# Seven products of a two-by-two block multiplication: one bank each, or three banks that collect the sums, with copies in between

## The chip, the cores and the metric

The program runs on one core of a Trainium2 chip. The metric is the device time in microseconds (us) of one execution; the verdict compares the medians of several executions. TensorE (PE) multiplies, VectorE (DVE) and ScalarE (ACT) work elementwise, GpSimd (POOL) helps with sums and splits, SyncE (SP) issues the transfers. Each of these works through its own instructions strictly in order.

## What is computed

One layer of a decoder block over 1024 tokens of width 1024, in float32: a gated feed-forward block, a token mixer, a second feed-forward block, each behind an RMS norm whose shift, scale and gate come from a condition vector `c` ("adaLN", nine vectors). Only the three wide input projections matter here:

```
def swiglu(h, w_in, w_out):
    a, b = jnp.split(h @ w_in, 2, axis=-1)
    return (jax.nn.silu(a) * b) @ w_out
...
q, f, i, og, u, ga, gb = jnp.split(h @ w_in, IN_SPLITS, axis=-1)   # the mixer
...
u = ua * jax.nn.sigmoid(ub)                                         # its convolution branch
merged = jax.nn.sigmoid(ga) * y_a + jax.nn.sigmoid(gb) * y_b        # its gates
```

## The kernel before

Every float32 operand is split in two parts (`parts`): a high one, a cast by ScalarE (L90), and a low one, what is left, a subtraction by VectorE (L91). A product of 128 by 128 weights and 512 columns is three matmuls (`mmw`, L232 to L234): high by high, high by low, low by high.

`paired` computes the wide input projections `h @ w_in` of both feed-forward blocks and of the mixer's u, ga and gb columns. For one pair of column blocks f (128 columns of a and of b) and all 1024 tokens it is a two by two block product, done with seven multiplications in place of eight. Each of the seven is a `product` of 4 x 3 matmuls, 128x512 each. The first two f's of a loop (`fs`) are done in the plain way while the operands come in ("warm"); the other f's, 20 in each feed-forward block and 14 in the mixer, run one after the other.

- `prepare(f)`: SyncE loads two raw tiles (`ra`, 512 KB each); they are split and combined into seven weight operands w11, w12, w22, ws1 to ws4 in the pool `wp`. The combinations (L306, L251) are made in place in the raw tiles. `prepare` of the next f stands in the program ahead of the seven products of this f.
- The seven products p1 to p7 go to seven of the eight PSUM banks in turn. Between them stand one copy (L321, ScalarE, p1 into a tile u) and six sums on VectorE (L323 to L335), each of which reads one bank.
- `emit` makes the result: in a feed-forward block a Silu on ScalarE (L360) and a product on VectorE (L361); `after` makes seven operands for the second half of the block out of each pair of f's (`combos`, four differences on VectorE, L354, and seven stores).
- In feed-forward 1 `after` also works off the adaLN vectors ("mod", L154): 56 rows of the matrix `ada_w`, four for an f. Each is loaded by SyncE (L147, 512 KB, tiles `ada`) into the pool `rp` of **three** raw tiles, the same pool from which `ra` comes, and multiplied and summed by one VectorE instruction over 1024 columns, in place. Its tile is free again when that has run.
- In the mixer's loop `after` starts the convolution, 31 VectorE instructions over 1024 columns for each of two channel blocks.

The order of the instructions on each engine is set when the program is built, by priorities: an instruction has the priority of its place in the code, and `defer(n)` moves it back by n. The same scheduler picks the free tile of a pool. At run time nothing is reordered.

Of the kernel before, what the change touches and what calls it, by code (L numbers as in the profile page):

```python
# [22 lines left out]
NKK = 11  # L23
# [17 lines left out]
class Block:  # L41
# [19 lines left out]
    @contextmanager  # L61
    def defer(self, n):

        keep = self.tc.cur_priority
        self.tc.cur_priority = keep + n
        yield
        self.tc.cur_priority = keep


    def half(self):  # L70
# [155 lines left out]
        self.split(t[:, 0, :], t[:, 1, :], src, eng)  # L226
        return t

    def mmw(self, ps, w, i, x, first, last):
        wh, wl = w[:, 0, i * P:(i + 1) * P], w[:, 1, i * P:(i + 1) * P]  # L230
        mm = self.nc.tensor.matmul
        mm(ps, wh, x[:, 0, :], start=first, stop=False)  # L232
        mm(ps, wh, x[:, 1, :], start=False, stop=False)  # L233
        mm(ps, wl, x[:, 0, :], start=False, stop=last)  # L234

# [6 lines left out]
    def paired(self, ctx, h, hctx, src, order, warm, emit, after, right, ready=()):  # L242


        nc = self.nc
        V, A = nc.vector, nc.scalar
        sub, add = ALU.subtract, ALU.add
        fs = order[:2]

        def tt(dst, a, b):  # L250
            V.tensor_tensor(dst, a, b, op=sub)  # L251

        def load(f):
            rs = []
            for b in range(2):
                rs.append(self.rp.tile([P, D], F32, tag="raw", name=self.nm("ra")))
                nc.sync.dma_start(rs[b], src(f, b))
            return rs

        self.part(ctx, wp=11, hq=8, bq=4)  # L260
        wop = lambda x: self.parts(x, self.wp, "w")
        hq = lambda x: self.parts(x, self.hq, "hq")


        ws, banks, b1 = {}, {}, dict(ready)

        def warm_load(f):
            ws[f] = [[self.parts(r[:, i * T:(i + 1) * T], self.wp, "w", nc.gpsimd) for i in range(2)] for r in load(f)]

        def warm_parts(hh, k):  # L270
            if (hh, k) not in b1:
                b1[hh, k] = self.parts(h[1][k], self.bq, "bq") if hh == 1 and k < 4 else self.parts(h[hh][k])

        def warm_mm(f, hh, k):
            if k == 0:
                banks[f, hh] = [self.acc() if f == fs[0] else self.bank() for _ in range(2)]
            for b in range(2):
                self.mmw(banks[f, hh][b], ws[f][b][k // 4], k % 4, b1[hh, k], k == 0, k == NK - 1)

        def warm_end(hh):  # L280
            for f in fs:
                emit(f, hh, *banks[f, hh], None)

        warm(fs, warm_load, warm_parts, warm_mm, warm_end)
        b11, b21, b22 = ([b1[hh, k0 + i] for i in range(4)] for hh, k0 in ((0, 0), (0, 4), (1, 4)))
        t1, t2, t3, t4 = [], [], [], []
        for i in range(4):
            x11, x12, x21, x22 = h[0][i], h[1][i], h[0][4 + i], h[1][4 + i]
            for o, x, y in ((x11, x12, x11), (x12, x22, x12), (x22, x22, x11), (x21, x21, x22)):
                nc.gpsimd.tensor_tensor(o, x, y, op=sub)  # L290
            t2.append(hq(x22))
            t3.append(hq(x12))
            t1.append(self.parts(x11))
            t4.append(self.parts(x21, self.bq, "bq"))
        hctx.close()
        self.part(ctx, right=True, **right)

        def product(ps, w, xs):
            for i in range(4):
                self.mmw(ps, w, i, xs[i], i == 0, i == 3)  # L300

        def prepare(f):
            ra, rb = load(f)
            a11, a12, a21, a22 = ra[:, :T], ra[:, T:], rb[:, :T], rb[:, T:]
            w11, w12, w22 = wop(a11), wop(a12), wop(a22)
            V.tensor_tensor(a22, a21, a22, op=add)  # L306
            tt(a21, a11, a21)
            tt(a11, a22, a11)
            tt(a12, a12, a11)
            ws2, ws3, ws1, ws4 = wop(a11), wop(a21), wop(a22), wop(a12)  # L310
            return w11, w12, w22, ws1, ws2, ws3, ws4

        ops = None
        for n, f in enumerate(order):
            if f not in fs:
                w11, w12, w22, ws1, ws2, ws3, ws4 = ops if ops else prepare(f)
                ops = prepare(order[n + 1]) if n + 1 < len(order) else None
                p1, p2, p3, p4, p5, p6, p7 = [self.acc() if (7 * n + i) % 2 == 0 else self.bank() for i in range(7)]
                product(p1, w11, b11)
                c11, c21, c22, u = (self.piece() for _ in range(4))  # L320
                A.copy(u, p1)  # L321
                product(p2, w12, b21)
                V.tensor_tensor(c11, p2, u, op=add)  # L323
                product(p3, ws2, t2)
                V.tensor_tensor(u, p3, u, op=add)
                product(p4, ws3, t3)
                V.tensor_tensor(c22, p4, u, op=add)
                product(p5, w22, t4)
                V.tensor_tensor(c21, p5, c22, op=add)
                emit(f, 0, c11, c21, c21)  # L330
                product(p6, ws1, t1)
                V.tensor_tensor(c22, p6, c22, op=add)
                V.tensor_tensor(u, p6, u, op=add)
                product(p7, ws4, b22)
                V.tensor_tensor(u, p7, u, op=add)  # L335
                emit(f, 1, u, c22, c22)
            after(n, f)
        return b1

    def piece(self):  # L340
# [3 lines left out]
    def ffn(self, h, hctx, w_in, w_out, gate, warm, residual, norm, done, between=None):  # L344
# [6 lines left out]
        gs = {f: [] for f in order}  # L351

        def tt(dst, a, b):
            V.tensor_tensor(dst, a, b, op=sub)  # L354
# [1 line left out]
        def swiglu(f, hh, a, b, dst):  # L356
            s = self.half()
            if dst is None:
                dst = self.half()
            A.activation(s, a, AF.Silu)  # L360
            V.tensor_tensor(dst, b, s, op=ALU.mult)  # L361
            gs[f].append(dst)

        def combos(i):

            (x11, x12), (x21, x22) = gs[i], gs[NKK + i]
# [12 lines left out]
            put(6, c4)  # L379
# [12 lines left out]
        with ExitStack() as ctx:  # L392
# [54 lines left out]
            us = []  # L447
# [227 lines left out]
    def run(self):  # L675
# [113 lines left out]
        def mix_in(f, hh, x, y, dst):  # L789
            sx = x if dst is not None else self.half()  # L790
            A.activation(sx, x, AF.Sigmoid)
            if f >= NH:
                sy = y if dst is not None else self.half()
                A.activation(sy, y, AF.Sigmoid)
                for b, s in enumerate((sx, sy)):
                    nc.sync.dma_start(self.g_dram[b][hh][f - NH], s)
            elif f in CONV_EARLY:
                if hh == 0:
# [221 lines left out]
```

## Time and profile before

| | |
|---|---|
| median of 3 runs | 2473.54 us (2471.91 to 2474.42) |
| the profiled execution, its own time | 2474.77 us |
| its span, first to last instruction | 2473.0 us |
| granted TensorE clock, mean | 0.994 |

The span is 1.8 us shorter than the time of the same execution; that difference lies around the instructions and is the same for every version. In the profile, "busy" of an engine is the time in which it executes; "idle before" a row is the time the engine stood still just ahead of it, with what ended the wait.

### The profile page before, as it was taken

The page shows a single profiled execution, that of the slowest core. Times are in us where ns is not written, and L with a number is a line of the kernel's source. Part 1 is how long each engine was busy: PE and PEld are TensorE (multiplying, and loading weights), DVE is VectorE, ACT ScalarE, POOL GpSimd, SP SyncE. Part 2 cuts the span into 40 slices and gives each one's busy share as a digit, 9 for nine tenths or more (in the row PEclk, how much of TensorE's full clock was granted, in tenths as well). Part 3 has the DMA queues.
Part 4 walks back from the last instruction along what each step waited for, and adds up shares of the span by engine and source line. Part 5 has one row for each costly group of instructions (what it writes and reads, how often), then busy time and mean ns, then how long its engine had stood idle before and what let it go on. Part 6 is the DMA issues. An engine that isn't in the chain of part 4 may idle for free.

```text
span 2473.0 us, 30875 instructions
## 1 busy us (share of the span) xinstructions
PE 2411.6 (98%) x11320; PEld 2002.2 (81%) x11320; DVE 2012.1 (81%) x3010; ACT 943.4 (38%) x1679; POOL 115.9 (5%) x77
## 2 busy tenths in 40 slices
PE   4999999999999999999999999999999999999997
PEld 2788878888878888788888888888888888888886
DVE  8989899678889999799999877575668777775977
ACT  4522233344644333333333335453343333324443
POOL 3300000000060000000000000000050000000000
PEclk9999999999999999999999999999999999999999
DMA  7256565595523323211111112674523233328743
GB/s 276 67 189 209 196 208 187 175 340 179 168 85 119 107 78 113 94 64 61 60 43 64 56 56 82 232 265 157 159 81 124 90 107 106 103 86 291 273 130 124
DMA packets 139975, 346.46 MB, mean 140 GB/s; under 512 B 15536, under 2 KB 15664, under 8 KB 139824
## 3 DMA queue, kind: packets, MB, share of 16 engines
q1 hardware_dynamic: 139680, 343.97, 41.3%
q8 instruction: 89, 1.46, 0.2%
q10 hardware_dynamic: 144, 0.52, 0.1%
q14 instruction: 62, 0.51, 0.1%
HBM read 266.31 MB, written 78.12 MB: 139 GB/s over the span
## 4 chain that ended last, share of the span: by engine, by line
PE 90%; DVE 6%; DMA 2%; issue 1%; ACT 1%; POOL 0%; SPq 0%; DVEq 0%; ACTq 0%
PE pa L233 10%; PE pa L234 10%; PE pa L232 10%; PE pb L234 10%; PE pb L233 10%; PE pb L232 9%; PE pa L106 8%; PE pa L104 8%; PE pa L105 8%; PE pb L577 4%; DMA ada<-in_ada_w_dram 1%; DVE ada L154 1%; PE pb L616 1%; PE pb L601 1%; PE pb L636 1%
## 5 line engine op out<-in xcount | busy, mean ns | idle before, releaser
L90 ACT CAST w<-ra 128x512 fp32r<-128x512 f32 x402 | 238.4, 619 | 435.6 <-PE pb L234 120.0
L104 PE MATMUL pa<-h,wh 128*128 128x512 f32 x896 | 355.4, 397 | 1.5 <-ACT wh L90 1.5
L106 PE MATMUL pa<-h,wl 128*128 128x512 f32 x896 | 353.7, 395 | 1.8 <-DVE wl L91 1.8
L105 PE MATMUL pa<-h,wh 128*128 128x512 f32 x896 | 353.1, 394 | 0.0
L543 DVE SCALAR_TENSOR_TENSOR uc<-u,par,uc 128x1023 f32<-128x1023 f32 (+14 forms) x240 | 303.2, 1263 | 2.7
L91 DVE TENSOR_TENSOR w<-ra,w 128x512 fp32r<-128x512 f32 x378 | 255.0, 690 | 10.6 <-ACT w L90 9.4
L232 PE MATMUL pa<-h,w 128*128 128x512 f32 x504 | 198.4, 396 | 5.0 <-ACT h L90 3.4
L234 PE MATMUL pb<-h,w 128*128 128x512 f32 x504 | 198.0, 393 | 4.7 <-POOL w L91 4.7
L233 PE MATMUL pa<-h,w 128*128 128x512 f32 x504 | 199.2, 395 | 2.7 <-DVE h L91 2.7
L234 PE MATMUL pa<-h,w 128*128 128x512 f32 x504 | 198.1, 393 | 0.0
L106 PEld LDWEIGHTS pa<-h,wl 128*128 128x128 f32 x896 | 168.6, 188 | 36.2 <-DVE wl L91 2.5
L233 PE MATMUL pb<-h,w 128*128 128x512 f32 x504 | 197.5, 392 | 0.0
L104 PEld LDWEIGHTS pa<-h,wh 128*128 128x128 f32 x896 | 168.7, 188 | 35.3 <-ACT wh L90 2.3
L232 PE MATMUL pb<-h,w 128*128 128x512 f32 x504 | 196.3, 390 | 0.0
L105 PEld LDWEIGHTS pa<-h,wh 128*128 128x128 f32 x896 | 168.9, 188 | 33.1 <-issue 0.7
L90 ACT CAST ob<-br 128x512 fp32r<-128x512 f32 x154 | 95.7, 622 | 186.2 <-PE pb L234 80.1
L90 ACT CAST wh<-raw 128x1024 fp32r<-128x1024 f32 x80 | 84.0, 1052 | 207.2 <-PE pa L105 194.4
L91 DVE TENSOR_TENSOR ob<-br,ob 128x512 fp32r<-128x512 f32 x154 | 106.7, 694 | 64.8 <-ACT ob L90 64.1
L233 PE MATMUL pa<-ob,oa 128*128 128x512 f32 x352 | 137.4, 390 | 1.3 <-DVE ob L91 1.3
L232 PE MATMUL pa<-ob,oa 128*128 128x512 f32 x352 | 137.0, 389 | 0.0
L234 PE MATMUL pa<-ob,oa 128*128 128x512 f32 x352 | 137.0, 389 | 0.0
L360 ACT ACTIVATE s<-c 128x512 f32<-128x512 f32 x80 | 50.6, 633 | 186.1 <-DVE c L335 128.3
(233 smaller groups left out, 5035.2 us busy)
## 6 DMA issues: line engine op xcount, KB each, us to landing
ra<-in_ffn_w_in_dram SPq DMA_DIRECT2D x88, 512.0 KB, 4.2
br<-bd SPq DMA_DIRECT2D x154, 256.0 KB, 3.1
bd<-c SPq DMA_DIRECT2D x146, 256.0 KB, 2.0
ada<-in_ada_w_dram SPq DMA_DIRECT2D x72, 512.0 KB, 4.5
ar<-in_ffn_w_out_dram SPq DMA_DIRECT2D x88, 256.0 KB, 4.5
ra<-in_mix_w_in_dram SPq DMA_DIRECT2D x32, 512.0 KB, 3.7
raw<-in_mix_w_in_dram SPq DMA_DIRECT2D x32, 512.0 KB, 3.5
ar<-in_ffn_w_out_dram SPq DMA_DIRECT2D x22, 512.0 KB, 5.2
```

What stands on the lines that cost most here:

```text
L90: self.nc.scalar.copy(hi, src)
L91: (eng or self.nc.vector).tensor_tensor(lo, src, hi.bitcast(F32), op=ALU.subtract)
L104: mm(ps, wh, x[:, 0, :], start=first, stop=False)
L105: mm(ps, wh, x[:, 1, :], start=False, stop=False)
L106: mm(ps, wl, x[:, 0, :], start=False, stop=last)
L154: self.nc.vector.scalar_tensor_tensor(raw, raw, 1.0, self.cs, op0=ALU.mult, op1=ALU.mult, accum_out=dst)
L232: mm(ps, wh, x[:, 0, :], start=first, stop=False)
L233: mm(ps, wh, x[:, 1, :], start=False, stop=False)
L234: mm(ps, wl, x[:, 0, :], start=False, stop=last)
L360: A.activation(s, a, AF.Silu)
L543: V.scalar_tensor_tensor(uc[:, j:], u[:, :S - j], cw(KC - 1 - j), uc[:, j:], op0=ALU.mult, op1=ALU.add)
L577: mm(ps[:, i * 64:(i + 1) * 64], ch(k, i), two(ch(qa, i))[:, :, 1, :], start=True, stop=True)
```

## The change

Three banks serve one f in place of seven. `chain` collects w11, then ws2 on top, then ws3, then w22; `low` collects ws1, then ws4 on top; `left` holds w12. Partial sums that are wanted by themselves are copied out by ScalarE in between (p1, u2 from `chain`, p6 from `low`), so that three copies and three sums stand where one copy and six sums stood. A product that adds to a bank which has been copied waits for that copy. The last product of an f, w22 (`rest`), is done one f later, behind the w12 product of the next f, and its `emit` reads the bank itself. The pool `wp` shrinks from 11 to 9 tiles and a pool `w22` of 2 is added. Copies and the last sum are moved ahead in priority by 200 (`sooner`). The lists of results (`gs`) become dictionaries since the halves now come in another order; that and two like edits in the mixer add no instruction.

```
+    def sooner(self, n):
+
+        return self.defer(-n)
...
-    def mmw(self, ps, w, i, x, first, last):
+    def mmw(self, ps, w, i, x, first, last, more=False):
+
         wh, wl = w[:, 0, i * P:(i + 1) * P], w[:, 1, i * P:(i + 1) * P]
+        kw = {"skip_group_check": True} if more else {}
...
-        self.part(ctx, wp=11, hq=8, bq=4)
+        self.part(ctx, wp=9, w22=2, hq=8, bq=4)
...
-        def product(ps, w, xs):
-            for i in range(4):
-                self.mmw(ps, w, i, xs[i], i == 0, i == 3)
+        def product(ps, w, xs, more=False):
+            for i in range(4):
+                self.mmw(ps, w, i, xs[i], not more and i == 0, i == 3, more)
...
-            w11, w12, w22 = wop(a11), wop(a12), wop(a22)
+            w11, w12, w22 = wop(a11), wop(a12), self.parts(a22, self.w22, "w22")
             V.tensor_tensor(a22, a21, a22, op=add)
             tt(a21, a11, a21)
             tt(a11, a22, a11)
             tt(a12, a12, a11)
-            ws2, ws3, ws1, ws4 = wop(a11), wop(a21), wop(a22), wop(a12)
+            ws1, ws2, ws4, ws3 = wop(a22), wop(a11), wop(a12), wop(a21)
             return w11, w12, w22, ws1, ws2, ws3, ws4
...
-                p1, p2, p3, p4, p5, p6, p7 = [self.acc() if (7 * n + i) % 2 == 0 else self.bank() for i in range(7)]
-                product(p1, w11, b11)
-                c11, c21, c22, u = (self.piece() for _ in range(4))
-                A.copy(u, p1)
-                product(p2, w12, b21)
-                V.tensor_tensor(c11, p2, u, op=add)
-                product(p3, ws2, t2)
-                V.tensor_tensor(u, p3, u, op=add)
-                product(p4, ws3, t3)
-                V.tensor_tensor(c22, p4, u, op=add)
-                product(p5, w22, t4)
-                V.tensor_tensor(c21, p5, c22, op=add)
-                emit(f, 0, c11, c21, c21)
-                product(p6, ws1, t1)
-                V.tensor_tensor(c22, p6, c22, op=add)
-                V.tensor_tensor(u, p6, u, op=add)
-                product(p7, ws4, b22)
-                V.tensor_tensor(u, p7, u, op=add)
-                emit(f, 1, u, c22, c22)
-            after(n, f)
...
+            chain, left, low = self.acc(), self.bank(), self.bank()
+            p1, p6, u2, c11, c12, c22 = (self.piece() for _ in range(6))
+            product(chain, w11, b11)
+            with self.sooner(200):
+                A.copy(p1, chain)
+            product(left, w12, b21)
+            V.tensor_tensor(c11, left, p1, op=add)
+            if rest:
+                rest()
+            product(low, ws1, t1)
+            with self.sooner(200):
+                A.copy(p6, low)
+            product(chain, ws2, t2, True)
+            with self.sooner(200):
+                A.copy(u2, chain)
+            product(low, ws4, b22, True)
+            V.tensor_tensor(c12, low, u2, op=add)
+            product(chain, ws3, t3, True)
+            with self.sooner(200):
+                V.tensor_tensor(c22, chain, p6, op=add)
+            emit(f, 1, c12, c22, c22)
+
+            def rest(n=n, f=f, chain=chain, w22=w22, c11=c11):
+                product(chain, w22, t4, True)
+                emit(f, 0, c11, chain, c11)
+                after(n, f)
+
+        rest()
```

What that does to the order on three engines, in the loop of feed-forward 1:

SyncE, before: the transfers of about one f. `ada` are rows of the adaLN matrix, `ra` the raw weights of the next f, `bd` stores of operands for later. In the built program `ada_294`, `295`, `297`, `320` and `321` have one and the same place in memory of the three of the pool, `ada_296` another.

```order
L147 DMA ada_294_1857<-in_ada_w_dram 128x1024
L369 DMA bd03_213<-c_260_1602 128x512
L147 DMA ada_295_1860<-in_ada_w_dram 128x1024
L147 DMA ada_296_1863<-in_ada_w_dram 128x1024
L147 DMA ada_297_1866<-in_ada_w_dram 128x1024
L257 DMA ra_298_1869<-in_ffn1_w_in_dram 128x1024
L257 DMA ra_299_1871<-in_ffn1_w_in_dram 128x1024
```

SyncE, after: the same stretch. Here `ada_274`, `275`, `276`, `277`, `301`, `302` and `303` all have one place; the next eight (`304` to `354`) have another one.

```order
L151 DMA ada_274_1738<-in_ada_w_dram 128x1024
L151 DMA ada_275_1741<-in_ada_w_dram 128x1024
L388 DMA bd03_213<-c_243_1534 128x512
L151 DMA ada_276_1744<-in_ada_w_dram 128x1024
L151 DMA ada_277_1747<-in_ada_w_dram 128x1024
L263 DMA ra_279_1807<-in_ffn1_w_in_dram 128x1024
L263 DMA ra_280_1809<-in_ffn1_w_in_dram 128x1024
L151 DMA ada_301_1900<-in_ada_w_dram 128x1024
```

What moved: the kinds and their number are as before; the places that the scheduler picked have changed, so that of eight loads in a row seven go into a tile that the load before them has used.

VectorE, before: from one adaLN row to two others. `c` are pieces of the result, `w` operands, `pa` and `pb` banks.

```order
L154 SCALAR_TENSOR_TENSOR ada_295_1860,mod3_90<-ada_295_1860,cs_303 128x1024
L325 TENSOR_TENSOR c_288_1756<-pb_280_1736,c_288_1756 128x512
L91 TENSOR_TENSOR w_277_1731<-ra_269_1705,w_277_1731 128x512
L154 SCALAR_TENSOR_TENSOR ada_296_1863,mod3_90<-ada_296_1863,cs_303 128x1024
L327 TENSOR_TENSOR c_287_1755<-pa_281_1737,c_288_1756 128x512
L154 SCALAR_TENSOR_TENSOR ada_297_1866,mod3_90<-ada_297_1866,cs_303 128x1024
L329 TENSOR_TENSOR c_286_1754<-pb_282_1738,c_287_1755 128x512
L361 TENSOR_TENSOR c_286_1754<-c_286_1754,s_289_1810 128x512
```

VectorE, after: the whole stretch between two adaLN rows in an f that also has the four differences; `ada_301` stands right ahead of the first row shown.

```order
L335 TENSOR_TENSOR c_294_1842<-pb_289_1837,c_291_1839 128x512
L373 TENSOR_TENSOR c_298_1886<-c_272_1696,c_245_1536 128x512
L373 TENSOR_TENSOR c_245_1536<-c_245_1536,c_243_1534 128x512
L380 TENSOR_TENSOR c_270_1694<-pa_264_1688,s_297_1883 128x512
L95 TENSOR_TENSOR w22_283_1817<-ra_280_1809,w22_283_1817 128x512
L373 TENSOR_TENSOR c_299_1887<-c_272_1696,c_245_1536 128x512
L312 TENSOR_TENSOR ra_280_1809<-ra_280_1809 128x512
L373 TENSOR_TENSOR c_300_1888<-c_270_1694,c_299_1887 128x512
L257 TENSOR_TENSOR ra_280_1809<-ra_279_1807,ra_280_1809 128x512
L95 TENSOR_TENSOR w_284_1824<-ra_280_1809,w_284_1824 128x512
L257 TENSOR_TENSOR ra_279_1807<-ra_280_1809,ra_279_1807 128x512
L158 SCALAR_TENSOR_TENSOR ada_302_1903,mod3_90<-ada_302_1903,cs_303 128x1024
```

What moved: the sums that read a bank (six for an f) are three, and the rows `ada` stand where the scheduler found room: one stretch has eleven instructions between two of them.

ScalarE, before: three casts for the next f, the copy of p1 of this f, a cast, a Silu.

```order
L90 CAST w_468_2832<-ra_463_2815 128x512
L90 CAST w_469_2835<-ra_464_2817 128x512
L90 CAST w_470_2838<-ra_464_2817 128x512
L321 COPY c_482_2866<-pa_472_2844 128x512
L90 CAST w_471_2841<-ra_463_2815 128x512
L360 ACTIVATE s_483_2920<-c_479_2863 128x512
```

ScalarE, after: the three copies of one f (L333 p1, L340 p6, L343 u2), and between them casts for the next f: w22, ws1, ws2.

```order
L333 COPY c_444_2761<-pa_441_2758 128x512
L94 CAST w22_436_2739<-ra_433_2731 128x512
L94 CAST w_437_2746<-ra_433_2731 128x512
L340 COPY c_445_2762<-pb_443_2760 128x512
L94 CAST w_438_2749<-ra_432_2729 128x512
L343 COPY c_446_2763<-pa_441_2758 128x512
```

What moved: p1's copy stands ahead of the casts that need VectorE, p6's copy behind the cast of ws1, u2's copy behind that of ws2.

## Rows read from the trace of the kernel before

**Rows 1.** The page, part 1: busy time, share of span, instructions of each engine.
```profile
PE 2411.6 (98%) x11320; PEld 2002.2 (81%) x11320; DVE 2012.1 (81%) x3010; ACT 943.4 (38%) x1679; POOL 115.9 (5%) x77
```

**Rows 2.** Stages: length; busy PE, PEld, DVE, ACT, POOL; clock, DMA share, GB/s.
```profile
100.00:470.00 370.00, 367.97 (x1615) 302.36 (x1615) 333.26 (x554) 110.94 (x196) 0.00 (x0) 1.00 0.57 190
710.00:1020.00 310.00, 307.97 (x1355) 253.94 (x1354) 279.61 (x371) 116.48 (x197) 27.20 (x17) 1.00 0.29 98
1825.00:2245.00 420.00, 420.00 (x1853) 347.21 (x1851) 320.27 (x483) 144.60 (x244) 28.23 (x18) 1.00 0.31 103
```

**Rows 3.** TensorE in order of time: first and last matmul of one product.
```profile
328.29 0.39 PE L232 MATMUL pa<-h,w 128*128 128x512 f32 x1
...
330.79 0.39 PE L234 MATMUL pa<-h,w 128*128 128x512 f32 x1
```

**Rows 4.** TensorE in order of time: a bubble in the loop of feed-forward 1.
```profile
349.82 0.39 PE L234 MATMUL pb<-h,w 128*128 128x512 f32 x1
350.96 0.50 PE L232 MATMUL pa<-h,w 128*128 128x512 f32 x1 [0.75 <-ACT c L321]
```

**Rows 5.** TensorE's waits in feed-forward 1's loop: waited for, us in total, times, longest.
```profile
PE pa L232 <- ACT c L321: 1.5, 2, 0.8
```

**Rows 6.** ScalarE in order of time, ahead of the same bubble.
```profile
348.77 1.66 ACT L90 CAST w<-ra 128x512 fp32r<-128x512 f32 x3 [1.97 <-DVE ra L251]
350.33 0.58 ACT L321 COPY c<-pa 128x512 f32<-128x512 f32 x1
```

**Rows 7.** VectorE in order of time, in the loop of feed-forward 1.
```profile
332.03 0.69 DVE L323 TENSOR_TENSOR c<-pa,c 128x512 f32<-128x512 f32 x1
332.63 1.22 DVE L154 SCALAR_TENSOR_TENSOR ada<-ada,cs 128x1024 f32<-128x1024 f32 x1
...
335.68 1.23 DVE L154 SCALAR_TENSOR_TENSOR ada<-ada,cs 128x1024 f32<-128x1024 f32 x1 [0.62 <-DMA ada<-in_ada_w_dram]
...
338.43 1.22 DVE L154 SCALAR_TENSOR_TENSOR ada<-ada,cs 128x1024 f32<-128x1024 f32 x1 [0.92 <-DMA ada<-in_ada_w_dram]
```

**Rows 8.** The DMA queue of SyncE in the same stretch.
```profile
332.15 0.33 SPq L147 DMA_DIRECT2D ada<-in_ada_w_dram  x1
333.89 0.33 SPq L147 DMA_DIRECT2D ada<-in_ada_w_dram  x1
335.09 2.18 SPq L257 DMA_DIRECT2D ra<-in_ffn_w_in_dram  x2
```

**Rows 9.** VectorE: first and last of 33 adaLN rows, four pairs of f's apart.
```profile
234.97 1.21 DVE L154 SCALAR_TENSOR_TENSOR ada<-ada,cs 128x1024 f32<-128x1024 f32 x1
...
394.80 1.21 DVE L154 SCALAR_TENSOR_TENSOR ada<-ada,cs 128x1024 f32<-128x1024 f32 x1
```

**Rows 10.** First f of feed-forward 1: TensorE's start, ScalarE's wait for a load.
```profile
98.69 0.39 PE L232 MATMUL pa<-h,w 128*128 128x512 f32 x1
...
111.43 0.62 ACT L90 CAST w<-ra 128x512 fp32r<-128x512 f32 x1 [4.95 <-DMA ra<-in_ffn_w_in_dram]
```

**Rows 11.** First f of the mixer: TensorE's start, VectorE's first sum.
```profile
747.00 0.39 PE L232 MATMUL pa<-h,w 128*128 128x512 f32 x1
...
757.39 0.68 DVE L323 TENSOR_TENSOR c<-pb,c 128x512 f32<-128x512 f32 x1
```

**Rows 12.** First f of feed-forward 2: TensorE's start, ScalarE, VectorE's next operand.
```profile
1864.14 0.39 PE L232 MATMUL pa<-h,w 128*128 128x512 f32 x1
...
1870.77 0.58 ACT L321 COPY c<-pa 128x512 f32<-128x512 f32 x1
...
1872.54 0.68 DVE L306 TENSOR_TENSOR ra<-ra 128x512 f32<-128x512 f32 x1
...
1875.66 2.18 ACT L90 CAST w<-ra 128x512 fp32r<-128x512 f32 x4 [4.31 <-DVE ra L251]
```

**Rows 13.** TensorE where the mixer loop gives way to the heads.
```profile
1014.90 0.50 PE L104 MATMUL pa<-h,wh 128*128 128x512 f32 x1 [1.18 <-ACT wh L90]
...
1017.45 0.50 PE L106 MATMUL pa<-h,wl 128*128 128x512 f32 x1 [0.57 <-DVE wl L91]
```

More of the change, by code (lines that the diff above doesn't have):

```diff
@@ L227, in parts @@
         return t
-    def mmw(self, ps, w, i, x, first, last):
+    def mmw(self, ps, w, i, x, first, last, more=False):
         wh, wl = w[:, 0, i * P:(i + 1) * P], w[:, 1, i * P:(i + 1) * P]
+        kw = {"skip_group_check": True} if more else {}
         mm = self.nc.tensor.matmul
-        mm(ps, wh, x[:, 0, :], start=first, stop=False)
-        mm(ps, wh, x[:, 1, :], start=False, stop=False)
-        mm(ps, wl, x[:, 0, :], start=False, stop=last)
+        mm(ps, wh, x[:, 0, :], start=first, stop=False, **kw)
+        mm(ps, wh, x[:, 1, :], start=False, stop=False, **kw)
+        mm(ps, wl, x[:, 0, :], start=False, stop=last, **kw)
     def paired(self, ctx, h, hctx, src, order, warm, emit, after, right, ready=()):
@@ L309, in prepare @@
             tt(a12, a12, a11)
-            ws2, ws3, ws1, ws4 = wop(a11), wop(a21), wop(a22), wop(a12)
+            ws1, ws2, ws4, ws3 = wop(a22), wop(a11), wop(a12), wop(a21)
             return w11, w12, w22, ws1, ws2, ws3, ws4
-        ops = None
+        ops, rest = None, None
         for n, f in enumerate(order):
-            if f not in fs:
-                w11, w12, w22, ws1, ws2, ws3, ws4 = ops if ops else prepare(f)
-                ops = prepare(order[n + 1]) if n + 1 < len(order) else None
-                p1, p2, p3, p4, p5, p6, p7 = [self.acc() if (7 * n + i) % 2 == 0 else self.bank() for i in range(7)]
-                product(p1, w11, b11)
-                c11, c21, c22, u = (self.piece() for _ in range(4))
-                A.copy(u, p1)
-                product(p2, w12, b21)
-                V.tensor_tensor(c11, p2, u, op=add)
-                product(p3, ws2, t2)
-                V.tensor_tensor(u, p3, u, op=add)
-                product(p4, ws3, t3)
-                V.tensor_tensor(c22, p4, u, op=add)
-                product(p5, w22, t4)
-                V.tensor_tensor(c21, p5, c22, op=add)
-                emit(f, 0, c11, c21, c21)
-                product(p6, ws1, t1)
-                V.tensor_tensor(c22, p6, c22, op=add)
-                V.tensor_tensor(u, p6, u, op=add)
-                product(p7, ws4, b22)
-                V.tensor_tensor(u, p7, u, op=add)
-                emit(f, 1, u, c22, c22)
-            after(n, f)
@@ new lines, in paired @@
+            if f in fs:
+                after(n, f)
+                continue
+            w11, w12, w22, ws1, ws2, ws3, ws4 = ops if ops else prepare(f)
+            ops = prepare(order[n + 1]) if n + 1 < len(order) else None
+            chain, left, low = self.acc(), self.bank(), self.bank()
[4 more added lines that the diff above has]
+            product(left, w12, b21)
@@ L338, in paired @@
+            emit(f, 1, c12, c22, c22)
+            def rest(n=n, f=f, chain=chain, w22=w22, c11=c11):
+                product(chain, w22, t4, True)
+                emit(f, 0, c11, chain, c11)
+                after(n, f)
+        rest()
         return b1
@@ L350, in ffn @@
         order = [f for i in range(NKK) for f in (i, NKK + i)]
-        gs = {f: [] for f in order}
+        gs = {f: {} for f in order}
         def tt(dst, a, b):
@@ L361, in swiglu @@
             V.tensor_tensor(dst, b, s, op=ALU.mult)
-            gs[f].append(dst)
+            gs[f][hh] = dst
         def combos(i):
-            (x11, x12), (x21, x22) = gs[i], gs[NKK + i]
+            (x11, x12), (x21, x22) = ((gs[j][0], gs[j][1]) for j in (i, NKK + i))
             c3, c2, c4 = (self.piece() for _ in range(3))
@@ L792, in mix_in @@
             if f >= NH:
-                sy = y if dst is not None else self.half()
+                sy = y if dst is not None and hh else self.half()
                 A.activation(sy, y, AF.Sigmoid)
@@ L797, in mix_in @@
             elif f in CONV_EARLY:
-                if hh == 0:
+                if f not in us:
                     us[f] = self.role("u")
```

## Prediction

> **What bounds the kernel now.** I read the page's engines first: TensorE is busy for 98% of the span [rows 1], so the end moves only where TensorE idles or works more. Then the three loops by stage: busy 367.97 of 370 us, 307.97 of 310 and 420.00 of 420 [rows 2]. The change leaves every matmul in place, 84 for an f, so the gain is at most the few idle us; a loss comes from every wait that it puts ahead of a matmul. One product is 12 matmuls; 328.29 to 330.79 is eleven steps [rows 3], so 0.227 us a step, 2.73 us a product, 19.1 us an f and 38.2 us a pair of f's.
>
> Next, where TensorE waits now. In the first loop matmuls start at 349.82 and 350.96 [rows 4], 0.91 us more than a step, behind a copy at ScalarE, the only wait of this kind, 1.5 us in all [rows 5]. The copy at 350.33 stood behind casts which waited for VectorE [rows 6], and it belongs to the product that began at 328.29 [rows 3]: some 19 us late, and only then does a matmul wait. Seven of eight banks in turn are what absorbs this. The lateness comes from VectorE, whose adaLN rows wait for their loads [rows 7].
>
> **The adaLN chain, feed-forward 1.** A tile of the pool of three is loaded again once its row is done. A row starts at 332.63 and the next load of its tile is issued at 333.89 [rows 7, 8]: 1.26 us. A load alone took from 332.15 to 335.68, 3.53 us; with two `ra` loads behind it, 333.89 to 338.43, 4.54 us [rows 7, 8]. So a link (row, issue, landing) is 4.79 us, or 5.80 when crowded. Before, 32 intervals last 234.97 to 394.80, 39.95 us for eight [rows 9]: already more than 38.2, which the banks hide.
>
> After, seven of eight loads take the place of the row just before (five of eight before), as the order of SyncE shows. For a pair of f's, from its first row: three links of 4.79 and a crowded one, 20.2; then the stretch with eleven instructions on VectorE, 1.15 + 11 x 0.60 = 7.75, to 27.9 (0.60 is 332.63 − 332.03; a row lasts 1.22, of which the last 0.07 or so overlap the next, as in a sum that lasts 0.69 [rows 7]); a link, to 32.7; the row in the other place, whose load is issued behind a row and three more instructions, 27.9 + 2.95 + 4.54 = 35.4; a crowded link, 41.2. That is 3.0 us above TensorE's 38.2. With no link crowded it is 38.2 (no loss), at 39.95 as before 1.75, with one more crowded 42.2. Now TensorE must follow: u2's copy stands behind the cast of ws2, which waits for VectorE, and ws3 adds to the same bank after one product of 2.73 us; the absorbing 19 us are gone. Of the seven groups of eight rows, I count five that run regularly: 5 x 3.0 = 15, less 1 for VectorE being early at first: **+14** (bounds 0 to 5 x 4.0 = 20). I take the crowded value since the `ra` loads stand behind the same rows in the order.
>
> By the Trainium skill, "SBUF — State Buffer", section "The DMA setup-cost knee", 512 KB would take about 2 us plus bytes over 436 GB/s, an estimate of 3.2 us. With 1.26 + 3.2 for every link the pair comes to 36.2 us and the chain would cost nothing; the trace shows 3.53 and 4.54, so I go by the trace.
>
> **First f's.** Here the casts for the next f come late, and a copy behind one is late with it. Feed-forward 1: p6's copy stands behind w22's cast, which waits for a load until 111.43 [rows 10]; done at 112.5 (0.52 for the cast, a third of 350.33 − 348.77 [rows 6], 0.58 for the copy). The product ws4, which adds to its bank, is due four products behind the start, 98.69 + 10.9 = 109.6: **+3**. Feed-forward 2: TensorE begins at 1864.14; in before the copy is done ahead of the four casts that VectorE delays (1870.77 against 1875.66) [rows 12]; after it p1's copy stands behind two of these, which need the instruction at 1872.54 and three pitches: 1874.3, with cast and copy 1875.4. ws2 is due at 1864.14 + 8.2 = 1872.3: **+3.1**. Mixer: p6's copy waits behind a sigmoid of VectorE's first sum, begun at 757.39 [rows 11]; it ends with sum, activation and copy at about 759.3; due 747.00 + 10.9 = 757.9: **+1.4**. These three may each be 0 if the scheduled loads come earlier, or 5 us if two copies are late: bounds 0 to 12 for the sum of 7.5.
>
> **What goes away.** The bubbles of the first loop: 2.03 us idle by the stage [rows 2], a little more by the starts (0.91 where 0.75 is listed [rows 4]): **−2.5**. Where the mixer gives way to the heads TensorE waits 1.18 and 0.57 and smaller ones for the heads' casts [rows 13]; the w22 product of the last f now stands last in the loop, 2.73 us later than the rest that VectorE and ScalarE have done: **−2** (0 to −2.8).
>
> **Edits at nothing.** VectorE saves three sums an f, 0.60 each, and ScalarE gains two copies, 0.58 each [rows 6, 7]. ScalarE is busy 38% of the span and VectorE 81% [rows 1], so both lie beside TensorE; if that cover were gone, two copies at 20 f's of a loop would be 23 us. In the mixer and feed-forward 2 there are no adaLN rows. VectorE has 279.61 of 310 and 320.27 of 420 us of work there [rows 2], less three sums an f. Laying out the order of after at 0.60 and 0.52 a row, p6's copy is done about 1.0 us and u2's about 1.4 us before the matmul that waits for it (estimates from these pitches). Cost 0. The pools keep their total; six pieces an f in place of four find free tiles in the order shown, and w22's own pool only lets it live an f longer.
>
> A rule speaks against the change. The Trainium skill, "Perfetto Trace Analysis", section "Matmuls", says that independent groups of matmuls should rotate through different PSUM banks so that one's evacuation overlaps the next one's matmuls. Rows 5 and 6 agree: it is the rotation that lets a copy be 19 us late for 0.75 us of idle.
>
> **The sum.** 14 + 7.5 − 2.5 − 2 = +17 on the profiled execution's 2474.77 us: 2491.8. The median shown is 1.2 us lower: **2490 us**.
>
> **Rivals.** (1) *The chain doesn't bind.* If loads land as alone (38.2 us a pair), TensorE waits only in the first f's: 7.5 − 2.5 − 2 = +3, about 2476.5. For it: landing alone is 3.53; against it: 39.95 for eight rows before [rows 9], with fewer dependent loads. It decides at 38.2 us a pair. (2) *Faster.* VectorE's three sums saved in each f (1.8 us of 19.1) bring operands early enough that every copy is in time, in the first f's too: −4.5, about 2469. For it: VectorE is 90% busy in the first loop [rows 2], so 3.6 us a pair is much. Against it: its rows wait for loads, not for work, and the three first f's have no earlier sum to save. It decides if the copies of p6 and u2 end before their dues (109.6, 757.9 and the next). (3) *The copies are late in every f.* The margins of 1.0 and 1.4 us in the mixer and feed-forward 2 are estimates; each us beyond them costs 1 us in each of 13 + 19 f's, so a lateness of 2 us would add about 32, 2520. For it: ScalarE works strictly in order, with Silu and sigmoids between the casts; against it: TensorE never waits for ScalarE in feed-forward 2's loop now, 420.00 of 420.
>
> **How the numbers follow.** A measurement tells 0.2%, 5 us, from no change. Forecast 0.68; rival (1) 0.16; rival (2) 0.09; rival (3) 0.07. The likeliest is 2490. Its own range: chain 0 to 20 and first f's 0 to 12 don't fail together; 2480 to 2499. To leave out no more than 2 in 10 I go down to rival (1) and a little into (2): 2472 to 2499. Faster 0.09; same 0.16; slower 0.75.
>
> **What would show it.** Right: in feed-forward 1's loop TensorE idles about 3 us per pair of f's, ended by the copy at L343 (or L340), and eight adaLN rows take about 41 us, VectorE waiting for `ada`; one bubble of about 3 us in the first f of each feed-forward block and 1.4 us in the mixer's; busy all through in the mixer's and feed-forward 2's loops; the wait ahead of the heads gone. Wrong: eight rows in 38 us; bubbles in every f of the other loops; or first f's with no bubble, since the casts' data came earlier than I place them.

## The result, and the profile after

The changed kernel takes 2529.01 us (median; 2526.38 to 2530.24, 4 runs) against 2473.8 us: 1.0223 times as long (95% interval 1.0211 to 1.0236), 55 us more. The forecast was 2490, with 2472 to 2499 as its range: right in its sign, and far too small.

The page of the kernel after, part 1 (its span, and busy time, share and instructions of each engine):

```profile
span 2527.9 us, 30618 instructions
PE 2431.1 (96%) x11320; PEld 2012.5 (80%) x11320; DVE 1893.9 (75%) x2794; ACT 994.9 (39%) x1787; POOL 116.9 (5%) x77
```

Against [rows 1], TensorE has the same 11320 matmuls and yet is busy for 19.5 us more. So the 54.9 us of added span fall into 19.5 us in which matmuls ran slower and 35.4 us of idle. Where they lie is seen from the first matmul of each stage (start, duration, instruction; in brackets the wait ahead of it and what ended it):

```profile
509.77 0.80 PE L238 MATMUL pa<-ob,oa 128*128 128x512 f32 x1 [6.32 <-ACT ob L94]
...
727.73 0.39 PE L238 MATMUL pa<-h,w 128*128 128x512 f32 x1
...
1050.30 0.39 PE L108 MATMUL pa<-h,wh 128*128 128x512 f32 x1
...
1851.86 0.39 PE L238 MATMUL pa<-h,w 128*128 128x512 f32 x1
...
2291.98 0.80 PE L238 MATMUL pa<-ob,oa 128*128 128x512 f32 x1 [6.44 <-ACT ob L94]
```

The same five matmuls stand in the trace of before at 483.67, 696.85, 1014.90, 1818.73 and 2244.94. Differences of neighbours give the stages:

| stage (to the first matmul of the next) | before, us | after, us | difference |
|---|---|---|---|
| start and feed-forward 1's projections | 483.67 | 509.77 | +26.1 |
| second half of feed-forward 1 | 213.18 | 217.96 | +4.8 |
| the mixer's projections | 318.05 | 322.57 | +4.5 |
| heads, convolution, merge | 803.83 | 801.56 | −2.3 |
| feed-forward 2's projections | 426.21 | 440.12 | +13.9 |
| second half of feed-forward 2, end | 228.06 | 235.92 | +7.9 |

Four things make this up. A "seam" is the point at which the next stage begins.

**The chain of adaLN rows.** VectorE in the loop of feed-forward 1, rows eight apart:

```profile
239.65 1.23 DVE L158 SCALAR_TENSOR_TENSOR ada<-ada,cs 128x1024 f32<-128x1024 f32 x1 [0.31 <-DMA ada<-in_ada_w_dram]
...
280.64 1.22 DVE L158 SCALAR_TENSOR_TENSOR ada<-ada,cs 128x1024 f32<-128x1024 f32 x1 [0.55 <-DMA ada<-in_ada_w_dram]
...
322.29 1.22 DVE L158 SCALAR_TENSOR_TENSOR ada<-ada,cs 128x1024 f32<-128x1024 f32 x1 [0.67 <-DMA ada<-in_ada_w_dram]
```

Eight rows take 41.0 and 41.65 us (the next two groups, to 364.54 and 405.63, 42.25 and 41.09), against 39.95 before [rows 9] and 41.2 forecast. VectorE's waits for these loads in the loop (waited for: us in total, times, longest) are 57.0 us where they were 20.4 in before:

```profile
DVE ada L158 <- DMA ada<-in_ada_w_dram: 57.0, 46, 3.9
```

TensorE now feels it. Its waits from 100 to 480 us, in place of the one row [rows 5]:

```profile
PE pb L238 <- ACT c L340: 11.0, 6, 2.5
PE pa L238 <- ACT c L343: 3.8, 4, 1.2
```

One of these stalls, VectorE first, then ScalarE, then TensorE's matmul:

```profile
224.45 1.23 DVE L158 SCALAR_TENSOR_TENSOR ada<-ada,cs 128x1024 f32<-128x1024 f32 x1 [2.26 <-DMA ada<-in_ada_w_dram]
...
229.33 0.68 DVE L312 TENSOR_TENSOR ra<-ra 128x512 f32<-128x512 f32 x1
```

```profile
224.00 0.62 ACT L94 CAST w<-ra 128x512 fp32r<-128x512 f32 x1 [2.21 <-PE pa L240]
230.10 0.62 ACT L94 CAST w<-ra 128x512 fp32r<-128x512 f32 x1 [5.48 <-DVE ra L312]
230.63 0.58 ACT L340 COPY c<-pb 128x512 f32<-128x512 f32 x1
```

```profile
231.26 0.50 PE L238 MATMUL pb<-h,w 128*128 128x512 f32 x1 [1.86 <-ACT c L340]
```

VectorE's row at 224.45 has waited 2.26 us for its load, and VectorE has no gap from there to L312. The cast at 230.10 waits 5.48 us for that L312; the copy of p6 (L340) behind it ends just before 231.26, and the matmul that adds to that bank has waited 1.86 us. One of the ten waits above, 2.17 us before 111.6, belongs to the first f. In each of the other nine (0.55 to 2.51 us) the cast ahead of the late copy waits for VectorE (L312 or L257), in none for a load of `ra`; so a late `ra` is not what delays these copies. The prediction had u2's copy (L343) as the one that is mostly late; p6's has 11.0 of the 14.8 us, 2.2 of them in the first f.

**The seams that the prediction left out.** At 509.77 and 2291.98 TensorE has waited 6.32 and 6.44 us for the first operand of the second half. The end of feed-forward 1's loop, TensorE, SyncE's queue and ScalarE:

```profile
500.40 0.50 PE L238 MATMUL pa<-bq,w 128*128 128x512 f32 x1 [0.79 <-DVE c L348]
...
503.06 0.39 PE L240 MATMUL pa<-bq,w 128*128 128x512 f32 x1
```

```profile
502.78 2.35 SPq L388 DMA_DIRECT2D bd<-c  x3
505.22 0.39 SPq L423 DMA_DIRECT2D br<-bd  x1
506.01 1.04 SPq L388 DMA_DIRECT2D bd<-c  x2
507.11 2.02 SPq L423 DMA_DIRECT2D br<-bd  x3
```

```profile
509.10 0.62 ACT L94 CAST ob<-br 128x512 fp32r<-128x512 f32 x1 [8.17 <-DMA br<-bd]
```

The w22 product of the last f ends the loop (500.40 to 503.06 and 0.39). It waits 0.79 us for VectorE's last sum, since no other product stands between ws3 and w22 here. It reads t4, and t4 lies in the tiles `bq`; in the built programs the five tiles `br` of the second half lie over three of the four places. Ahead of `br` stand the stores `bd` of the last f, which wait for VectorE; then one `br` is issued at 505.22, three more behind other stores, and the first cast has waited 8.17 us for it. In before, w22 was the fifth of seven products, and the second half began at 483.67, one step behind the last product at 483.44. Behind the seam there is one more wait, since the next eight `br` stand behind eight loads of x in the queue (1.7 us here, 3.2 in feed-forward 2):

```profile
PE pa L238 <- ACT ob L94: 8.0, 2, 6.3
PE pa L238 <- DVE c L348: 0.8, 1, 0.8
```

**The clock.** Granted clock behind a short wait (212.7 us, 1.06 us idle before) and behind a seam; columns as in [rows 2]:

```profile
212.70:216.00 3.30, 3.22 (x14) 2.68 (x15) 2.94 (x6) 1.07 (x3) 0.00 (x0) 1.00 0.14 21
2292.00:2296.00 4.00, 4.00 (x9) 2.92 (x10) 2.00 (x3) 1.24 (x2) 0.00 (x0) 0.50 0.95 311
```

At 1.00 (2.4 GHz) 3.3 us hold 14 matmuls, at 0.50 (1.2 GHz) 4.0 us hold 9. Behind the waits of 2.17 us before 111.6, 1.86 before 231.3, 3.05 before 1908.6 and the two seams, the next 3.3 to 4.4 us have a mean granted clock of 0.61, 0.59, 0.50, 0.50 and 0.50. I take such stretches to be the 19.5 us; they were not added up one by one. The sum of the prediction had no term for them. The Trainium skill, "Perfetto Trace Analysis", section "Matmul Optimizations", says that the engine scales its power with use and that matmuls should run back to back; the rows agree.

**The first f's.** Feed-forward 2, ScalarE and TensorE: casts for the next f wait for VectorE, p1's copy (L333) stands behind them, and ws2's first matmul waits 3.05 us, as forecast (3.1).

```profile
1906.02 0.62 ACT L94 CAST w<-ra 128x512 fp32r<-128x512 f32 x1 [0.57 <-DVE ra L312]
1907.47 0.62 ACT L94 CAST w<-ra 128x512 fp32r<-128x512 f32 x1 [0.83 <-DVE ra L257]
1907.99 0.58 ACT L333 COPY c<-pa 128x512 f32<-128x512 f32 x1
```

```profile
1908.63 0.79 PE L238 MATMUL pa<-hq,w 128*128 128x512 f32 x1 [3.05 <-ACT c L333]
```

In feed-forward 1 it is 2.17 us (3 forecast): the cast of w22, behind which p6's copy stands, starts at 110.44 and not at 111.43. In the mixer p6's copy behind the sigmoid costs 1.6 us (1.4 forecast), and p1's copy 0.8, which was not forecast.

Idle, added up: chain 14.8 − 2.2 = 12.6, first f's 2.2 + 2.4 + 3.0 = 7.6, seams 12.8, waits in the second halves 4.9, w22 behind the last sum 3 x 0.8 = 2.4; less the bubbles (1.5 by [rows 5]) and the wait at the heads (2.0, [rows 13] and one of 0.28) that are gone: 36.8 against the 35.4 that the page gives.

### The profile page after: what moved, and what is told of

It reads as the page before. It is cut to its first block, busy times and chain, and to the rows that moved or that the text cites. A ratio compares the mean times of both kernels' runs of the same rounds, so it can differ in the third digit from the quotient of the medians.

```text
span 2527.9 us, 30618 instructions
## 1 busy us (share of the span) xinstructions
PE 2431.1 (96%) x11320; PEld 2012.5 (80%) x11320; DVE 1893.9 (75%) x2794; ACT 994.9 (39%) x1787; POOL 116.9 (5%) x77
## 4 chain that ended last, share of the span: by engine, by line
PE 77%; DVE 10%; DMA 8%; issue 3%; ACT 1%; POOL 1%; SPq 0%; DVEq 0%; ACTq 0%; POOLq 0%
PE pa L239 9%; PE pa L238 9%; PE pa L240 9%; PE pa L109 8%; PE pa L110 8%; PE pa L108 7%; PE pb L238 7%; PE pb L239 7%; PE pb L240 7%; DMA ada<-in_ada_w_dram 5%; PE pb L596 4%; DVE h L95 1%; DVE ada L158 1%; DVE w L95 1%; DVE hq L95 1%
## 5 line engine op out<-in xcount | busy, mean ns | idle before, releaser
L238 PE MATMUL pb<-h,w 128*128 128x512 f32 x720 | 283.6, 395 | 12.6 <-ACT c L340 12.6
L240 PE MATMUL pb<-h,w 128*128 128x512 f32 x720 | 283.4, 394 | 4.0 <-POOL w L95 4.0
L239 PE MATMUL pb<-h,w 128*128 128x512 f32 x720 | 283.4, 394 | 0.0
L95 DVE TENSOR_TENSOR w<-ra,w 128x512 fp32r<-128x512 f32 x378 | 255.9, 694 | 26.9 <-ACT w L94 23.9
L238 PE MATMUL pa<-hq,w 128*128 128x512 f32 x432 | 169.8, 393 | 7.7 <-ACT c L343 3.8
L238 PEld LDWEIGHTS pb<-h,w 128*128 128x128 f32 x720 | 136.8, 190 | 44.4 <-ACT c L340 15.9
L239 PE MATMUL pa<-hq,w 128*128 128x512 f32 x432 | 169.1, 391 | 0.0
L240 PE MATMUL pa<-hq,w 128*128 128x512 f32 x432 | 169.1, 391 | 0.0
L240 PEld LDWEIGHTS pb<-h,w 128*128 128x128 f32 x720 | 137.2, 191 | 34.1 <-POOL w L95 4.9
L239 PEld LDWEIGHTS pb<-h,w 128*128 128x128 f32 x720 | 137.0, 190 | 28.5
L238 PE MATMUL pa<-ob,oa 128*128 128x512 f32 x352 | 140.2, 398 | 17.6 <-ACT ob L94 17.6
```

Source lines behind the costliest of these rows:

```text
L95: (eng or self.nc.vector).tensor_tensor(lo, src, hi.bitcast(F32), op=ALU.subtract)
L238: mm(ps, wh, x[:, 0, :], start=first, stop=False, **kw)
L239: mm(ps, wh, x[:, 1, :], start=False, stop=False, **kw)
L240: mm(ps, wl, x[:, 0, :], start=False, stop=last, **kw)
```

## The experiments

The theory after the result: the 55 us are three causes that can each be taken away alone, the place of t4, the first f's and the chain of loads, with what follows each by the clock. The rival: three banks with copies in between cost something in every f, so that the waits come back elsewhere. Times are medians; differences to the changed kernel are taken from 2529.0. Where an edit adds lines, the line numbers behind it shift.

**t4_moved.** t1 and t4 change places.

```
-            t1.append(self.parts(x11))
-            t4.append(self.parts(x21, self.bq, "bq"))
+            t1.append(self.parts(x11, self.bq, "bq"))
+            t4.append(self.parts(x21))
```

> The operand t4 of the last product (w22) moves to the pool of the tiles h, and t1 to the tiles bq, on whose place the next stage's loads br land. Theory: the two feed-forward seams (6.7 and 6.8 us of idle, and the 4.8 and 7.9 us by which the second halves are longer) come from br having to wait for the last product, which reads t4; then both seams fall below 2 us, the second halves return to within 2 us of before, and the time is 22 to 28 us below after, about 2504. Rival: the second half waits for the last f's own results (its stores stand ahead of br in SyncE's queue, and its product must end first); then the seams stay above 5 us and the time changes by less than 5 us.

Measured: 2502.12 us, 26.9 less. SyncE's queue and TensorE at the seam:

```profile
489.24 2.23 SPq L423 DMA_DIRECT2D br<-bd  x5
...
500.53 2.34 SPq L388 DMA_DIRECT2D bd<-c  x3
```

```profile
500.80 0.39 PE L240 MATMUL pa<-h,w 128*128 128x512 f32 x1
501.03 0.39 PE L238 MATMUL pa<-ob,oa 128*128 128x512 f32 x1
```

Five `br` are issued at 489.24, ahead of the last stores, and the second half begins at 501.03 one step behind the last product. The stage of feed-forward 1 is 8.7 us shorter than in after, its second half 5.4, feed-forward 2 5.9 and its second half 8.2. The w22 product still waits 0.8 us for the last sum. One edit of where an operand lies gives back half of the loss; but the scheduler also put `br` ahead of the stores, and this run doesn't tell the two apart.

**stores_later** tells them apart: t4 stays, six of the seven stores of the last pair move back.

```
-            put = lambda n, t: nc.sync.dma_start(self.b_dram[n][i], t)
+            def put(n, t):
+                with self.defer(400 if i == NKK - 1 and n else 0):
+                    nc.sync.dma_start(self.b_dram[n][i], t)
```

> The change with six of the seven stores of the last pair of f's moved back in priority, so that the loads br, eight in a row, stand ahead of them and of the loads of x in SyncE's queue; t4 stays where it was. If the place of t4 alone holds br back: br is issued at the end of the last product, some 1.7 us earlier than in after (505.2 against 503.5), the seams fall from 6.3 to about 4.6 us, the second waits in the second halves (1.7 and 3.2 us) go since br no longer stands behind x, and the time falls by 8 to 14 us. If the stores ahead of br hold it back: the seams fall below 2 us and the time by 20 us or more.

Measured: 2514.55 us, 14.5 less, just above the 8 to 14 expected if the place of t4 holds `br` back. The seams are 3.77 and 3.87 us and the second waits are gone. `br` is issued at 504.69, where the last matmul (504.27 and 0.39) ends: it waits for that product, as SyncE's waits there say:

```profile
SPq L425 <- PE pa L240: 0.9, 1, 0.9
```

So by this run about 3.8 us of each seam is the place of t4 and 2.5 us the stores ahead of `br`.

**last_old.** The last f of each loop in the old way, seven banks.

```
+            if n == len(order) - 1:
+                p1, p2, p3, p4, p5, p6, p7 = [self.acc() if (7 * n + i) % 2 == 0 else self.bank() for i in range(7)]
...
+                continue
```

> Only the last f of each of the three loops is done in the old way, seven banks. Theory: as for t4, the seams vanish, 22 to 28 us less, another 1 us in each feed-forward loop (w22 no longer waits for the last sum of its bank), and the seam from the mixer to the heads gets back its 1.5 to 3 us: about 2503. Rival, that the whole second half is slower for another reason (its operands or places): the seams vanish but the second halves stay 5 to 8 us longer, about 2514.

Measured: 2507.74 us, 21.3 less, 5 us above what was expected. Both second halves start without a wait and are as long as in before (213.1 and 227.9 us), so the rival falls. At the heads the wait comes back, and larger: 2.90 us against 1.18 [rows 13].

**first_last_old.** The first f of each loop as well (the edit is shown against last_old).

```
-            if n == len(order) - 1:
+            if n in (2, len(order) - 1):
```

> The first and the last f of each loop in the old way. Theory: beside the seams the waits of the first f's go (2.3, 2.7 and 3.2 us idle, and about 2.5 us each in the two feed-forward ones where matmuls run at 0.427 us instead of 0.227 behind them), 11 to 13 us below the version with only the last f in the old way: about 2491. Rival: the first f's wait for their operands whatever the banks, or the second f of the loop waits in their place; then less than 4 us below.

Measured: 2497.44 us, 10.3 below last_old (11 to 13 expected). By stage feed-forward 1 is 4.7 us shorter, the mixer 1.7 and feed-forward 2 2.9. In the mixer a wait of 1.2 us turns up at the second f, so there the rival's part holds.

**ada_place.** A fourth tile, for every other adaLN row.

```
-            raw = self.mod_load(j, k, self.rp, "raw")
+            raw = self.mod_load(j, k, *((self.ap, "ap") if k % 2 else (self.rp, "raw")))
...
-            self.paired(ctx, h, hctx, lambda f, b: w_in[f, b], order, warm, swiglu, after, dict(cq=14))
+            self.paired(ctx, h, hctx, lambda f, b: w_in[f, b], order, warm, swiglu, after, dict(cq=14, **({"ap": 1} if between else {})))
```

> Every other adaLN row gets a fourth tile of its own, so that a load no longer follows on the row just before. Theory (chain of row, issue and landing): feed-forward 1's loop loses its periodic waits, eight rows take 38 us as TensorE's pair of f's does, and the time falls by 14 to 19 us (idle 14 and the lower clock behind the longer waits 4), about 2512. Rival (VectorE's work and the order of copies and casts alone): the waits stay and less than 5 us are gained, 2525 or more.

Measured: 2523.93 us, 5.1 less. That is nearest to its rival (less than 5 us), but the trace shows that the edit did not do what it was meant to. VectorE's waits from 100 to 440 us:

```profile
DVE ada L158 <- DMA ada<-in_ada_w_dram: 47.5, 37, 5.0
DVE c L335 <- PE pb L240: 11.3, 6, 4.0
```

They are 47.5 us instead of 57.0: the scheduler, which now had one more place, moved the rows closer together, several at once, and VectorE also waits for TensorE. So the run says nothing against the chain, nor for it.

**noload_after** and **noload_before** take the loads away instead of their place.

```
-            raw = self.mod_load(j, k, self.rp, "raw")
+            if not hasattr(self, "one"):
+                self.one = self.mod_load(j, k, self.ap, "ap")
+            raw = self.one
...
```

55 of the 56 loads of the loop are left out, so the adaLN vectors are not the right ones. The one tile lies in a pool of its own, and a factor in the row's instruction is 0.125 in place of 1.0.

> The 56 adaLN rows of the loop of feed-forward 1 are computed from one tile that is loaded once (the other loads are left out, and the adaLN vectors are not those of the reference); VectorE's rows stay in number and shape. Theory (what delays VectorE, the casts and with them the copies in feed-forward 1 is that rows wait for their loads): the periodic waits of TensorE go, 14 us of idle and some 4 us at the lower clock, 17 us below after, about 2512; the waits of the first f stay. Rival (VectorE's work alone, or the order of copies behind casts): more than half of the waits stay, 2520 or more.

> The kernel before with the same rows from one tile. Theory: only its three bubbles go, 2 to 3 us, about 2471, since eight banks hide the rest. Rival: nothing changes.

Measured: 2507.65 us, 21.4 less than after; and 2471.22 us, ratio to before 0.9991 (0.9982 to 1.0001). In noload_after, TensorE's waits from 100 to 480 us and VectorE's longest in total from 100 to 440 us:

```profile
PE pb L240 <- ACT c L342: 3.2, 2, 2.4
```

```profile
DVE c L337 <- PE pb L242: 35.4, 9, 4.0
```

VectorE has all its rows and now waits for TensorE, 35.4 us; TensorE waits 3.2 us in two places, 2.4 of them in the first f, where it waited 14.8. So it is the loads, and not VectorE's work or the order of the copies alone. The run takes away the loads with everything that they do to the queue and the pool; that it is the chain over one tile is read from the rows, not from this run. Before has the same loads and loses 2.6 us by them, not clear of no change, though VectorE waits for them there too (20.4 us); that fits the seven banks in turn. Here the rule of the Trainium skill that the prediction cited ("Perfetto Trace Analysis", section "Matmuls") has its price: the loads cost 21 us without the rotation, though with their rows in another order than before.

**ada_queue.** The loads of these rows are issued by GpSimd.

```
-            raw = self.mod_load(j, k, self.rp, "raw")
+            raw = self.mod_load(j, k, self.rp, "raw", self.nc.gpsimd)
```

> The adaLN loads of the loop are issued by GpSimd and no longer stand in SyncE's queue, where stores that wait for VectorE and the loads ra stand around them; tiles stay as they are. If SyncE's order delays them: at least 6 us less, 2522 or below. If only the chain through the tile (row, issue, landing) does: within 4 us of after.

Measured: 2558.35 us, 29 more, which neither theory expected. GpSimd's issues and VectorE's rows:

```profile
201.59 0.53 POOL L151 DMA_DIRECT2D ada<-in_ada_w_dram  x1 [6.04 <-DVE ada L158]
206.90 0.53 POOL L151 DMA_DIRECT2D ada<-in_ada_w_dram  x1 [4.79 <-DVE ada L158]
```

```profile
199.95 1.23 DVE L158 SCALAR_TENSOR_TENSOR ada<-ada,cs 128x1024 f32<-128x1024 f32 x1 [0.52 <-DMA ada<-in_ada_w_dram]
...
205.26 1.23 DVE L158 SCALAR_TENSOR_TENSOR ada<-ada,cs 128x1024 f32<-128x1024 f32 x1 [0.90 <-DMA ada<-in_ada_w_dram]
...
236.09 1.22 DVE L158 SCALAR_TENSOR_TENSOR ada<-ada,cs 128x1024 f32<-128x1024 f32 x1 [3.04 <-DMA ada<-in_ada_w_dram]
...
281.60 1.23 DVE L158 SCALAR_TENSOR_TENSOR ada<-ada,cs 128x1024 f32<-128x1024 f32 x1 [1.89 <-DMA ada<-in_ada_w_dram]
```

From a row's start to the issue it is 201.59 − 199.95 = 1.64 us (1.26 by SyncE [rows 7, 8]), and 3.67 to the next row. Eight rows take 45.5 us (236.09 to 281.60). A longer link and a longer loop go together, as they would if the chain sets its pace; between 41.0 and 45.5 us for eight, five to seven groups give an estimate of 22 to 32 us, and 29 were measured. But the tiles did not stay as they were, as had been expected: in the built program the rows change their place every four rows and not every eight, and other instructions stand between them. So the run doesn't show that the longer link alone costs the 29 us.

**all_mended.** t4 moved, the first f old (and not the last), loads by GpSimd: the edits above together.

> The change with t4 moved, the first f in the old way and the adaLN loads issued by GpSimd. From the runs so far: 27 us (t4) and 10 us (first f) below after, and what the queue is worth: 2485 to 2492, still above before by the waits of feed-forward 1 and of the mixer's second f. Rival: with the stalls gone elsewhere the seams' gains are kept and it comes below before, 2470 or less.

Measured: 2526.84 us, a miss, since the queue, which had been expected to help or to do nothing, costs as just told. Both second halves start without a wait.

**sum_noload.** t4 moved, the first f old, and no loads.

> The change with t4 moved, the first f in the old way, and the adaLN rows from one tile loaded once (other loads left out). If the three causes add and nothing else costs: 2529 − 27 (t4) − 10 (first f) − 21 (loads) = 2471, the same as the kernel before with the loads left out, 2471.2. If the copies between products cost something in every f: 2480 or more. If the three overlap: above 2476.

Measured: 2478.45 us, 50.6 below after and 7 above noload_before. Each measured by itself, the three add up to 58.6, so they overlap by 8 us. Part of that can be seen: in the loop of feed-forward 1 TensorE still waits 1.6 us for copies of p6 and 1.2 for an operand of VectorE, where noload_after waited 3.2: with the loads gone, the old first f there only moves the wait on.

**mended_place.** t4 moved, the first f old, the fourth tile; the best version that has the change in all three loops and computes everything.

> The change with t4 moved, the first f in the old way and the fourth tile for every other adaLN row; the whole reference is computed. If the parts add: 2529 − 27 − 10 − 5 = 2487, above before by what is left of the chain in feed-forward 1. If the places of the rows come out otherwise in this order, 2480 to 2497.

Measured: 2492.27 us, 1.0076 times before (1.0061 to 1.0091). What is left of the chain, TensorE's waits in the loop of feed-forward 1 (the copies of u2 and p6):

```profile
PE pa L238 <- ACT c L368: 6.2, 3, 2.9
PE pb L238 <- ACT c L365: 6.0, 6, 2.5
```

**ffn1_old.** Feed-forward 1 in the old way, the change elsewhere, t4 moved, first f's old (the line is shown against first_last_old).

```
-            if n in (2, len(order) - 1):
+            if self.old or n == 2:
```

> Feed-forward 1 wholly in the old way; the change in the mixer and in feed-forward 2 alone, with t4 moved and the first f of each in the old way. If the banks cost only where the adaLN loads are: 2474 plus 2 to 4 in the mixer's loop, less 3 at the heads and their seam, 2471 to 2476. If three banks cost in every f: 2485 or more.

Measured: 2480.02 us, 1.0025 times before (1.0013 to 1.0036), 4 above the expectation (2471 to 2476). The seven runs lie between 2474.92 and 2483.09, the profiled one at 2475.51; what lengthens most of the others is not known. TensorE in the loop of feed-forward 2 and its only wait there:

```profile
1825.00:2245.00 420.00, 419.11 (x1846) 346.02 (x1845) 277.14 (x403) 161.50 (x283) 27.91 (x18) 1.00 0.30 104
```

```profile
PE pa L238 <- DVE c L373: 0.8, 1, 0.8
```

419.11 of 420 us are busy, where it was 420.00 [rows 2]. So three banks with copies cost next to nothing in an f where VectorE is in time, and they gain nothing either. No version with the change was faster than before.

The run also shows the place once more. Feed-forward 1 ends in the old order here, but t1, which p6 reads, now lies in `bq`. p6's last matmul starts at 477.72 (0.39), `br` waits for TensorE and is issued at 478.14, and the second half waits 1.16 us where before had none:

```profile
SPq L450 <- PE pa L240: 0.6, 1, 0.6
```

```profile
481.98 1.20 PE L238 MATMUL pa<-ob,oa 128*128 128x512 f32 x4 [1.16 <-ACT ob L94]
```

## Why the prediction was wrong

**The chain of loads** was right in its working: 41.2 us for eight rows forecast, 41.0 to 42.25 measured, 14 us of idle forecast, 12.6 measured; without the loads, 0.8 us of it is left. That five-of-eight against seven-of-eight dependent loads makes the difference to before was argued from the order; no run changed that alone. The count for before is loose, too: in the built program four of eight rows take the place of the row just before them, and a fifth that of the row before last. By the page cited there (the Trainium skill, "SBUF — State Buffer", section "The DMA setup-cost knee") a pair would have been 36.2 us and rival (1) would have held; the trace disagrees.

**The step that failed** is "What goes away": the w22 product as the last of the loop was followed to one of three places, the heads, where it covers something (−2, and the wait is gone as forecast). At the two feed-forward ends it was counted as nothing; measured are 6.32 and 6.44 us of idle there and 4.9 behind. I did not ask what the last product reads, what lies on that place next, and what stands behind the last f's stores. t4_moved shows what that was worth: 26.9 of the 55 us, clock included; stores_later got back 14.5 with t4 left in its place.

**A term was missing** for the clock: every wait was counted once, as idle. The page of after shows 19.5 us more of busy time for the same matmuls, a third of the loss, which I put down to the lower clock behind the waits. With it the chain of 12.6 us idle was worth 21 (noload_after), and the first f's 7.6 us of idle 10.3. In the loop of feed-forward 1 it can be seen by itself: from 239.65 to 405.63 four groups take 13.2 us more than 4 x 38.2, and 8.7 of them are idle.

**First f's**: 7.5 us forecast, 7.6 us of idle measured. That the sums agree so well is in part luck: feed-forward 1 was 0.8 us too high, and p1's copy in the mixer, 0.8 us, was not foreseen. **Bubbles of before**: 2.5 us forecast to go; noload_before is 2.6 us faster (not clear of no change), and in after larger waits behind late copies took their place. **Edits at nothing**: copies and sums in the middle of the mixer's and feed-forward 2's loops are free, as forecast (ffn1_old); rival (3) didn't occur. Rivals (1) and (2) fell with the chain.

## What to carry to other kernels

A product that is moved to the end of a loop takes its operands with it: look up which tiles of the next stage lie on their place, and which loads wait for it, at every place where the loop ends. In this kernel a rotation through seven banks hid late copies from the matmuls; before it is given up for fewer instructions, look for an engine that is late by more than one product, since its lateness then costs time in full. And a wait of TensorE of some us is priced with the slower matmuls behind it, not as idle alone.

## What the runs showed beside

With loads of 512 KB for the same three tiles issued by GpSimd instead of SyncE, and the order that the scheduler made of it, the link from row to row was 5.3 us (199.95 to 205.26) and the kernel 29 us longer, although GpSimd was idle in that loop. And one more tile made the scheduler pack rows more tightly, so that VectorE's wait for loads hardly fell (57.0 to 47.5 us); that its order is built for loads that come earlier than they do is a guess which no run tests.
